# The last token tile of a trunk's last down projection: its tail products by halves of the columns, with the sum and the square of each half behind it

## The chip, the core and the metric

The kernel runs on one core of one Trainium2 chip, as one program. The metric is the device time of one execution in microseconds, the median of the timed runs. A profiled execution of the same program gives the trace; its span runs from the first instruction to the last. TensorE is called PE, its weight loads PEld, VectorE DVE, ScalarE ACT, GpSimd POOL and SyncE SP.

## The reference

A trunk of two layers over 512 tokens and 1024 channels, in float32. Each layer is a token mixer and a SwiGLU FFN, and each of these four ends in a gated RMSNorm that is added to the running `x`. Only the last step of the last FFN matters here:

```python
def rms_norm(x, g):
    xf = x.astype(jnp.float32)
    y = xf * lax.rsqrt(jnp.mean(xf * xf, axis=-1, keepdims=True) + EPS)
    return (y * g.astype(jnp.float32)).astype(x.dtype)

def swiglu(h, w_gate, w_up, w_down):
    return (jax.nn.silu(h @ w_gate) * (h @ w_up)) @ w_down
...
        y = swiglu(h, ffn_w_gate[i], ffn_w_up[i], ffn_w_down[i])
        x = x + gate * rms_norm(y, ffn_post_g[i])
    return x
```

`D_FF` is 2816, so the down projection has a contraction of 22 tiles of 128. The mean of the squares runs over all 1024 columns of a token: no column of the output can be scaled before the last square of its token is in.

## The kernel before

Matrices are multiplied in float32r, each operand split into a high and a low part; a product is three matmuls (`mm3`: high by high, high by low, low by high). The last FFN is `Ffn.last` (line 1255). Its down projection works on pairs of contraction tiles (11 pairs) and on the columns in two passes: pass `q = 0`, then `q = 1`, 512 columns each. The 512 columns of a pass are two groups of 256 (`h`), since the columns are laid out as `(h q c)`: half `h`, pass `q`, 256 columns.

In each pass eight PSUM banks are open, `Z`, `W`, `X` and `Y` for two token groups `s` (256 tokens each). Six of the eleven pairs in pass 1 go through a seven-product scheme of Winograd's kind (`seven`), the others through plain products (`eight`). The sums `Z` and `W`, which several outputs share, go to the tile `u` in `common` (line 1326). The last three pairs of pass 1 (`NLAST = 3`) are plain, and are kept back as `tail`: they are multiplied token tile by token tile, after everything else. There are four token tiles of 128 tokens (`tt`): tile `tt` has the bank `X` (even) or `Y` (odd) of the group `s = tt // 2`. For one token tile the tail is 3 pairs × 2 contraction tiles × 3 matmuls = 18 matmuls of 128x512 into one bank.

Behind the tail of each tile in pass 1 comes its finish, in this order in the code: `whole` adds bank and `u` into `y` on DVE and squares `y` on ACT with a running sum (`sq`; the squared values go to `junk` and are not used); `rms` (line 467) makes the sum of pass 0, scaled, the bias of a square root (`ss`, a DVE operation on 128x1) and takes that root on ACT (`sd`); `weigh` multiplies the kept half of pass 0 and then the new half by the weights `G` (`z`); a reciprocal on DVE gives `r`; two DVE operations add `r` times each half to `x`; each is followed by a DMA of its half of `x` to the output on SP's queue.

What sets the order: in this part no order is written out by hand. Each engine runs its own instructions one after the other as they stand in the built program. Between engines the framework places semaphore waits from the regions of tiles that instructions read and write. The listings below show, in square brackets, on which engine's semaphore a row waits.

Of the kernel before, what the change touches and what calls it, by code (L numbers as in the profile page):

```python
# [8 lines left out]
F32 = mybir.dt.float32  # L9
# [4 lines left out]
P = 128  # L14
T = 512
NT = T // P
# [17 lines left out]
def trunk(ctx: ExitStack, tc: tile.TileContext, A: dict, out: bass.AP):  # L34
# [17 lines left out]
    def nm(s):  # L52
        uid[0] += 1
        return f"{s}_{uid[0]}"
# [65 lines left out]
    def mm3(o, lh, ll, rh, rl, start, stop):  # L120
        mm(o, lh, rh, start, False)
        mm(o, lh, rl, False, False)
        mm(o, ll, rh, False, stop)

    def load(dst, src):
        nc.sync.dma_start(out=dst, in_=src)
# [1015 lines left out]
    class Ffn:  # L1142
# [112 lines left out]
        def last(self, bg0):  # L1255

            self.units(bg0)
            G = ada["G", 3].rearrange("p (h q c) -> p h q c", h=2, q=2)
            kept = {}

            def operands(q, p):

                a = self.act[p]
                t = slot(F32R, "ah"), slot(F32R, "al")
                split(t[0][:], t[1][:], a[:])  # L1270

                def A(e, c):
                    return lambda s: [
                        u[:, c, s * 256 + e * P : s * 256 + e * P + P] for u in t
                    ]

                ops = {f"A{e + 1}{c + 1}": A(e, c) for e in range(2) for c in range(2)}
                if p not in SEVEN[q]:
                    return ops
                if p not in kept:  # L1280
                    f = slot(F32, "S", 4, 256)
                    kept[p] = f
                    v = a[:].rearrange("p c (s e t) -> p c s e t", s=2, e=2)
                    S1, S2, S3, S4 = [
                        f[:, i, :].rearrange("p (s t) -> p s t", s=2) for i in range(4)
                    ]
                    dve.tensor_tensor(S1, v[:, 0, :, 1, :], v[:, 1, :, 1, :], ALU.add)
                    dve.tensor_tensor(S2, S1, v[:, 0, :, 0, :], ALU.subtract)
                    dve.tensor_tensor(S3, v[:, 0, :, 1, :], v[:, 0, :, 0, :], ALU.subtract)
                    dve.tensor_tensor(S4, v[:, 1, :, 0, :], S2, ALU.subtract)  # L1290
                f = kept[p]
                g = slot(F32R, "Sh", 4, 256), slot(F32R, "Sl", 4, 256)
                split(g[0][:], g[1][:], f[:])

                def S(i):
                    return lambda s: [u[:, i, s * P : (s + 1) * P] for u in g]

                ops.update({f"S{i + 1}": S(i) for i in range(4)})
                return ops

            def eight(p, O, W, banks, s, es, start):

                w = [[t[:, 2 * c : 2 * c + 2, :] for t in W] for c in range(2)]
                for e in es:
                    for c in range(2):
                        h, l = O[f"A{e + 1}{c + 1}"](s)
                        o = banks["XY"[e], s][:].rearrange("p (h c) -> p h c", h=2)
                        mm3(o, h, l, w[c][0], w[c][1], start and c == 0, False)

            SUMS = (  # L1310
                ("Z", 0, "A11", "B11"), ("W", 0, "S1", "T1"), ("Z", 1, "S2", "T2"),
                ("W", 1, "S3", "T3"), ("X", 0, "A12", "B21"), ("X", 1, "S4", "B22"),
                ("Y", 0, "A22", "T4"),
            )

            def seven(O, W, banks, fresh):
                for n, i, a, b in SUMS:
                    for s in range(2):
                        h, l = O[a](s)
                        mm3(  # L1320
                            banks[n, s][:, i * 256 : (i + 1) * 256], h, l, *W[b],
                            (n, s) in fresh, False,
                        )
                        fresh.discard((n, s))

            def common(banks):

                us = []
                for s in range(2):
                    u = fpool.tile([P, 4, 256], F32, tag="f13", name=nm("u"))  # L1330
                    z = [banks["Z", s][:, i * 256 : (i + 1) * 256] for i in range(2)]
                    w = [banks["W", s][:, i * 256 : (i + 1) * 256] for i in range(2)]
                    act.activation(u[:, 0, :], z[0], AF.Copy)
                    dve.tensor_tensor(u[:, 3, :], z[1], u[:, 0, :], ALU.add)
                    dve.tensor_tensor(u[:, 1, :], w[0], u[:, 3, :], ALU.add)
                    dve.tensor_tensor(u[:, 2, :], w[1], u[:, 3, :], ALU.add)
                    dve.tensor_tensor(u[:, 3, :], w[0], u[:, 2, :], ALU.add)
                    us.append(u)
                return us

            def whole(us, banks, tt, q):

                s, e = tt // 2, tt % 2
                y = ys[q, s][:, e, :]
                u = us[s][:, 2 * e : 2 * e + 2, :].rearrange("p a c -> p (a c)")
                dve.tensor_tensor(y, banks["XY"[e], s][:], u, ALU.add)
                sq = small.tile([P, 1], F32, tag=f"sq{q}{tt}", bufs=1, name=nm("sq"))
                act.activation(junk[:, q * 512 : (q + 1) * 512], y, AF.Square, accum_out=sq[:])
                yv = y.rearrange("p (h c) -> p h c", h=2)
                return sq, yv  # L1350

            def weigh(yv, q, out=None):
                dve.tensor_tensor(yv if out is None else out, yv, G[:, :, q, :], ALU.mult)

            ys = {}
            half = {}
            xs = []
            O = operands(0, PAIRS[0][0])
            for q in range(2):
                banks = {(n, s): bank(n, "p" if n == "W" else "b") for n in "ZWXY" for s in range(2)}  # L1360
                fresh = set(banks)
                tail = []
                us = None
                for n, p in enumerate(PAIRS[q]):
                    W = wget(("wdn", q, p), 2)
                    now = O
                    if n + 1 < NF or q == 0:
                        O = operands(*((q, PAIRS[q][n + 1]) if n + 1 < NF else (1, PAIRS[1][0])))
                    if p in SEVEN[q]:
                        seven(now, W, banks, fresh)  # L1370
                        if p == [i for i in PAIRS[q] if i in SEVEN[q]][-1]:
                            us = common(banks)
                    elif q == 1 and n >= NF - NLAST:
                        tail.append((p, now, W))
                    else:
                        for s in range(2):
                            eight(p, now, W, banks, s, (0, 1), ("X", s) in fresh)
                            fresh -= {("X", s), ("Y", s)}
                    if q == 1 and 0 <= n - 3 < NT:
                        xs.append(x_load(n - 3))  # L1380
                    if q == 1 and n == NF - NLAST - 2:
                        sqrt_table()
                for s in range(2):
                    ys[q, s] = slot(F32, "y")
                for tt in range(NT):
                    for t in tail:
                        eight(*t, banks, tt // 2, (tt % 2,), False)
                    if q == 0:
                        half[tt] = whole(us, banks, tt, 0)
                        continue  # L1390
                    sq, yv = whole(us, banks, tt, 1)
                    sd, r = rms(sq[:], half[tt][0][:])
                    weigh(half[tt][1], 0)
                    z = fpool.tile([P, 768], F32, tag="e", name=nm("z"))[:, :512]
                    z = z.rearrange("p (h c) -> p h c", h=2)
                    weigh(yv, 1, z)
                    dve.reciprocal(r[:], sd[:])
                    x = xs[tt].rearrange("p (h q c) -> p h q c", h=2, q=2)
                    o = out[tt * P : (tt + 1) * P, :].rearrange("p (h q c) -> p h q c", h=2, q=2)
                    for i, t in enumerate((half[tt][1], z)):  # L1400
                        dve.scalar_tensor_tensor(
                            x[:, :, i, :], t, r[:, 0:1], x[:, :, i, :], ALU.mult, ALU.add
                        )
                        load(o[:, :, i, :], x[:, :, i, :])


    u4 = []
# [269 lines left out]
```

## Time and profile before

| | us |
|---|---|
| timed runs | 1106.73, 1106.87, 1106.84; median 1106.84 |
| the profiled execution, span | 1104.6 |
| median of the runs less that span | 2.2 |
| PE busy in the span | 1085.9 (98%) |
| DVE busy | 945.9 (86%) |
| ACT busy | 594.2 (54%) |
| mean granted PE clock (share of full speed) | 0.998 |

The profile lists no time for the profiled execution outside its span; a timed run is 2.2 us longer than the span, which is what lies around the first and the last instruction. PE is busy nearly always, so what counts at the end of the kernel is when PE ends, and what has still to run behind it. In the views a row of the timeline is start, duration, engine, line, operation, output and inputs. Nearly every operation goes through a helper, so line 109 is any matmul, line 71 any DVE operation and line 87 any ACT operation: the tile names tell them apart. A durations row by form reads shortest/median/longest in ns.

### The profile page before, as it was taken

To read this page: it belongs to the slowest core of one execution; us is meant where nothing else is said; L and a number is where in the kernel's file an instruction comes from. 1 tells how busy PE (TensorE), PEld (TensorE's weight loads), DVE (VectorE), ACT (ScalarE), POOL (GpSimd) and SP (SyncE) were. 2 spreads that over 40 slices of the span, in tenths; PEclk is the share of its full clock that TensorE was granted. 3 is DMA by queue.
4 is the path that set the end of the run, shared out by engine and by line. 5 is a ranking of instruction groups with operands and counts; after the bars stand their busy time and mean duration, and the time that the engine had idled before them with its cause. 6 is when DMAs were issued, how large, how long until landed. Compare 5 with 4: busy or idle time off the path is not lost.

```text
span 1104.6 us, 18512 instructions
## 1 busy us (share of the span) xinstructions
PE 1085.9 (98%) x7404; PEld 979.0 (89%) x7404; DVE 945.9 (86%) x1248; ACT 594.2 (54%) x982; POOL 29.5 (3%) x53
## 2 busy tenths in 40 slices
PE   6999999999999999999999999999999999999997
PEld 4787788788999999998888889988999999989996
DVE  4988999966989999989866967668979999899997
ACT  6554665665655555554243626426555555565662
POOL 0020100000000000000000000001000000000000
PEclk9999999999999999999999999999999999999999
DMA  8976434304433434359757465334334343333252
GB/s 302 370 226 217 142 116 133 125 11 152 157 112 131 162 119 146 132 197 351 272 191 256 144 205 196 96 116 155 128 117 155 128 159 102 110 115 96 77 187 81
DMA packets 51355, 176.38 MB, mean 160 GB/s; under 512 B 6074, under 2 KB 9146, under 8 KB 51268
## 3 DMA queue, kind: packets, MB, share of 16 engines
q1 hardware_dynamic: 48708, 166.81, 44.6%
q0 software_dynamic: 2560, 8.39, 2.1%
q8 instruction: 58, 0.95, 0.3%
q14 instruction: 29, 0.24, 0.1%
HBM read 164.69 MB, written 8.39 MB: 157 GB/s over the span
## 4 chain that ended last, share of the span: by engine, by line
PE 90%; DVE 4%; DMA 2%; ACT 2%; issue 1%; SPq 0%; DVEq 0%; ACTq 0%
PE r L109 32%; PE y L109 18%; PE pqk L109 7%; PE gu L109 6%; PE v L109 5%; PE X L109 4%; PE u L109 4%; PE Y L109 3%; PE av L109 2%; PE z L109 2%; PE tw L117 1%; PE tp L117 1%; PE Z L109 1%; PE W L109 1%; PE ab L109 1%
## 5 line engine op out<-in xcount | busy, mean ns | idle before, releaser
L87 ACT ACTIVATE wh<-raw 128x1024 fp32r<-128x1024 f32 (+1 forms) x112 | 115.7, 1038 | 130.5 <-PE y L109 39.4
L109 PE MATMUL r<-Sh,wh 128*128 128x256 f32 x608 | 168.1, 276 | 0.5 <-ACT e L87 0.5
L109 PE MATMUL r<-Sh,wl 128*128 128x256 f32 x608 | 167.9, 276 | 0.0
L109 PE MATMUL r<-Sl,wh 128*128 128x256 f32 x608 | 167.9, 276 | 0.0
L109 PE MATMUL y<-wh,as 128*128 128x512 f32 x480 | 149.9, 390 | 0.0
L178 DVE TENSOR_TENSOR wl<-raw,wh 128x1024 fp32r<-128x1024 f32 x87 | 105.8, 1222 | 48.2 <-ACT wh L87 47.6
L109 PEld LDWEIGHTS r<-Sh,wh 128*128 128x128 f32 x608 | 114.1, 188 | 1.0 <-ACT e L87 0.9
L109 PEld LDWEIGHTS r<-Sl,wh 128*128 128x128 f32 x608 | 114.1, 188 | 0.1
L109 PEld LDWEIGHTS r<-Sh,wl 128*128 128x128 f32 x608 | 114.1, 188 | 0.0
L109 PEld LDWEIGHTS y<-wh,as 128*128 128x128 f32 x480 | 90.0, 188 | 18.6
L71 DVE TENSOR_TENSOR wl<-f,wh 128x1024 fp32r<-128x1024 f32 x87 | 103.2, 1220 | 0.0
L87 ACT ACTIVATE wh<-f 128x1024 fp32r<-128x1024 f32 x87 | 91.8, 1055 | 15.3 <-DVE f L71 11.6
L87 ACT ACTIVATE e<-r 128x256 f32<-128x256 f32 x114 | 43.7, 385 | 101.8 <-PE r L109 100.8
L109 PE MATMUL y<-wl,as 128*128 128x512 f32 x240 | 93.7, 391 | 0.0
L109 PE MATMUL r<-hTh,wh 128*128 128x256 f32 x304 | 84.2, 277 | 0.2 <-DVE gu L71 0.2
L109 PE MATMUL r<-hTl,wh 128*128 128x256 f32 x304 | 84.0, 276 | 0.0
L109 PE MATMUL r<-hTh,wl 128*128 128x256 f32 x304 | 84.0, 276 | 0.0
L109 PE MATMUL r<-hTh,b 128*128 128x256 f32 x304 | 57.9, 276 | 0.0
L109 PEld LDWEIGHTS r<-hTh,wh 128*128 128x128 f32 x304 | 57.1, 188 | 0.9 <-DVE gu L71 0.9
L109 PEld LDWEIGHTS r<-hTh,wl 128*128 128x128 f32 x304 | 57.1, 188 | 0.0
L109 PEld LDWEIGHTS r<-hTl,wh 128*128 128x128 f32 x304 | 57.1, 188 | 0.0
L87 ACT ACTIVATE wh<-rawx 128x1024 fp32r<-128x1024 f32 x38 | 40.4, 1063 | 29.8 <-PE r L109 29.0
(262 smaller groups left out, 2937.1 us busy)
## 6 DMA issues: line engine op xcount, KB each, us to landing
rawada<-in_ada SPq DMA_DIRECT2D x80, 512.0 KB, 5.7
rawy<-in_wy SPq DMA_DIRECT2D x38, 512.0 KB, 4.6
rawx<-in_wx SPq DMA_DIRECT2D x38, 512.0 KB, 3.7
raw<-in_wdown SPq DMA_DIRECT2D x22, 512.0 KB, 5.4
raw<-in_wdn SPq DMA_DIRECT2D x22, 512.0 KB, 3.6
raw<-in_wqk SPq DMA_DIRECT2D x16, 512.0 KB, 3.9
ada<-in_ada0p SPq DMA_DIRECT2D x12, 512.0 KB, 6.3
raw<-in_wgu SPq DMA_DIRECT2D x12, 512.0 KB, 3.5
```

What stands on the lines that cost most here:

```text
L71: b = getattr(nc.vector, op)(*args, **kw)
L87: b = nc.scalar.activation(*args, **kw)
L109: b = nc.tensor.matmul(o, l, r, start=start, stop=stop, skip_group_check=True)
L117: last_tp[0] = nc.tensor.transpose(o, i, ident)
L178: last_low[0] = nc.vector.tensor_tensor(l[:], raw[:], h[:].bitcast(F32), ALU.subtract)
```

## The change

For the last token tile of pass 1 alone (`tt = 3`) a function of its own, `last_tile`, takes the place of the common path. It runs the tail for the first 256 columns, then the sum and the square of these, then the tail for the other 256 columns, then their sum and square. `eight` gets a place `at` and a width `n` within the bank for that. The sum of the first half's squares is added to that of pass 0 (one more 128x1 operation on DVE), and `rms` takes this as its first part. The weighing is done by halves too. The last part (`finish`) is moved to a function and is the same.

```diff
-            def eight(p, O, W, banks, s, es, start):
+            def eight(p, O, W, banks, s, es, start, at=0, n=2):
 
-                w = [[t[:, 2 * c : 2 * c + 2, :] for t in W] for c in range(2)]
+                w = [[t[:, 2 * c + at : 2 * c + at + n, :] for t in W] for c in range(2)]
...
-                        mm3(o, h, l, w[c][0], w[c][1], start and c == 0, False)
+                        mm3(o[:, at : at + n], h, l, w[c][0], w[c][1], start and c == 0, False)
...
+            def last_tile(tail, us, banks, tt):
+                s, e = tt // 2, tt % 2
+                y = ys[1, s][:, e, :].rearrange("p (h c) -> p h c", h=2)
+                z = fpool.tile([P, 768], F32, tag="e", name=nm("z"))[:, :512]
+                z = z.rearrange("p (h c) -> p h c", h=2)
+                sq = [half[tt][0]]
+                weigh(half[tt][1], 0)
+                for h in range(2):
+                    for t in tail:
+                        eight(*t, banks, s, (e,), False, h, 1)
+                    dve.tensor_tensor(
+                        y[:, h, :], banks["XY"[e], s][:, h * 256 : (h + 1) * 256],
+                        us[s][:, 2 * e + h, :], ALU.add,
+                    )
+                    part = small.tile([P, 1], F32, tag="sq13" if h else "sq0", bufs=1 if h else None, name=nm("sq"))
+                    act.activation(
+                        junk[:, 512 + h * 256 : 768 + h * 256], y[:, h, :], AF.Square,
+                        accum_out=part[:],
+                    )
+                    if h == 0:
+                        dve.tensor_tensor(part[:], part[:], sq[0][:], ALU.add)
+                    sq.append(part)
+                    dve.tensor_tensor(z[:, h, :], y[:, h, :], G[:, h, 1, :], ALU.mult)
+                sd, r = rms(sq[2][:], sq[1][:])
+                dve.reciprocal(r[:], sd[:])
+                finish(tt, z, r)
...
                 for tt in range(NT):
+                    if q == 1 and tt == NT - 1:
+                        last_tile(tail, us, banks, tt)
+                        continue
```

On PE, at the end of the third tile's tail and the start of the fourth's (`X` is the third tile's bank, `Y` the fourth's, `wh`/`wl` and `ah`/`al` the high and low parts of weights and activations), there stood before:

```order
L109 MATMUL X_11315<-wl_11779,ah_11786 128x512
L109 MATMUL X_11315<-wh_11778,al_11787 128x512
L109 MATMUL Y_11317<-wh_11650,ah_11718 128x512
L109 MATMUL Y_11317<-wl_11651,ah_11718 128x512
L109 MATMUL Y_11317<-wh_11650,al_11719 128x512
```

and in the middle of the fourth tile's tail, where its first half ends and its second begins, there stand now:

```order
L109 MATMUL Y_11317<-wl_11779,ah_11786 128x256
L109 MATMUL Y_11317<-wh_11778,al_11787 128x256
L109 MATMUL Y_11317<-wh_11650,ah_11718 128x256 [waits DVE_49]
L109 MATMUL Y_11317<-wl_11651,ah_11718 128x256
L109 MATMUL Y_11317<-wh_11650,al_11719 128x256
```

The 18 matmuls of 128x512 have become 36 of 128x256, with the weights and activations of the first 18 used over again by the other 18. The nineteenth waits for DVE; no matmul of this tail waited for another engine before. In the built program the count on which it waits is the one that DVE's sum of the first half brings.

On DVE, the end of the program, from the third tile's last part on (`x_11646` belongs to the third tile, `x_11709` to the fourth, `y_11297` is the half of pass 0), before:

```order
L71 SCALAR_TENSOR_TENSOR x_11646<-z_11887,r_11885,x_11646 128x2x256
L71 TENSOR_TENSOR y_11791<-Y_11317,u_11770 128x512 [waits PE_49]
L71 TENSOR_TENSOR z_11921<-y_11791,G_8534 128x512 [waits DVE_49]
L71 RECIPROCAL r_11919<-sd_11917 128x1 [waits Activation_49]
L71 SCALAR_TENSOR_TENSOR x_11709<-y_11297,r_11919,x_11709 128x2x256 [waits DMAHW3_49,DVE_49]
L71 SCALAR_TENSOR_TENSOR x_11709<-z_11921,r_11919,x_11709 128x2x256
```

and now:

```order
L71 SCALAR_TENSOR_TENSOR x_11646<-z_11887,r_11885,x_11646 128x2x256
L71 TENSOR_TENSOR y_11791<-Y_11317,u_11770 128x256 [waits PE_49]
L71 TENSOR_TENSOR z_11894<-y_11791,G_8534 128x256 [waits DVE_49]
L71 TENSOR_TENSOR sq_11915<-sq_11915,sq_11308 128x1 [waits Activation_49]
L71 TENSOR_SCALAR ss_11941<-sq_11915 128x1 [waits DVE_49]
L71 TENSOR_TENSOR y_11791<-Y_11317,u_11770 128x256 [waits PE_49]
L71 TENSOR_TENSOR z_11894<-y_11791,G_8534 128x256 [waits DVE_49]
L71 RECIPROCAL r_11945<-sd_11943 128x1 [waits Activation_49]
L71 SCALAR_TENSOR_TENSOR x_11709<-y_11297,r_11945,x_11709 128x2x256 [waits DMAHW3_49,DVE_49]
L71 SCALAR_TENSOR_TENSOR x_11709<-z_11894,r_11945,x_11709 128x2x256
```

The sum and the weighing have become two each. The scaling `ss`, which stood ahead of all four tails, stands between the two sums now, with the new 128x1 sum before it, and both wait for ACT's first square. The first sum stands behind the third tile's two operations on `x`, as the whole sum did.

On ACT, the last squares and roots, before:

```order
L87 ACTIVATE sd_11849<-sq_11845,ss_11847 128x1 [waits Activation_49]
L87 ACTIVATE junk,sq_11879<-y_11791 128x512 [waits DVE_49]
L87 ACTIVATE sd_11883<-sq_11879,ss_11881 128x1 [waits Activation_49]
L87 ACTIVATE junk,sq_11913<-y_11791 128x512 [waits DVE_49]
L87 ACTIVATE sd_11917<-sq_11913,ss_11915 128x1 [waits Activation_49]
```

and now:

```order
L87 ACTIVATE junk,sq_11879<-y_11791 128x512 [waits DVE_49]
L87 ACTIVATE sd_11883<-sq_11879,ss_11881 128x1 [waits Activation_49]
L87 ACTIVATE junk,sq_11915<-y_11791 128x256 [waits DVE_49]
L87 ACTIVATE junk,sq_11938<-y_11791 128x256 [waits DVE_49]
L87 ACTIVATE sd_11943<-sq_11938,ss_11941 128x1 [waits Activation_49]
```

One square has become two of half the width. POOL's and SP's queues hold the same operations in the same order as before, the two DMAs of the last tile's output at the end among them.

More of the change, by code (lines that the diff above doesn't have):

```diff
@@ L1353, in weigh, with finish @@
                 dve.tensor_tensor(yv if out is None else out, yv, G[:, :, q, :], ALU.mult)
+            def finish(tt, z, r):
+                x = xs[tt].rearrange("p (h q c) -> p h q c", h=2, q=2)
+                o = out[tt * P : (tt + 1) * P, :].rearrange("p (h q c) -> p h q c", h=2, q=2)
+                for i, t in enumerate((half[tt][1], z)):
+                    dve.scalar_tensor_tensor(
+                        x[:, :, i, :], t, r[:, 0:1], x[:, :, i, :], ALU.mult, ALU.add
+                    )
+                    load(o[:, :, i, :], x[:, :, i, :])
+            def last_tile(tail, us, banks, tt):
[16 more added lines that the diff above has]
+                        accum_out=part[:],
+                    )
+                    if h == 0:
[5 more added lines that the diff above has]
+                finish(tt, z, r)
             ys = {}
@@ L1397, in last @@
                     dve.reciprocal(r[:], sd[:])
[L1398 to L1404, printed above, removed]
+                    finish(tt, z, r)
     u4 = []
```

## The prediction

> **What bounds the kernel now.** I read the page's busy shares first, then the chain of waits over the last 35 us, then the timelines of PE, DVE and ACT there. The share first:
>
> ```profile
> PE 1085.9 (98%) x7404; PEld 979.0 (89%) x7404; DVE 945.9 (86%) x1248; ACT 594.2 (54%) x982; POOL 29.5 (3%) x53
> ```
>
> PE has some 19 us without work in 1104.6, so a matmul more or a wait on PE is time, unless it falls where PE is idle. The chain that ended last (start, us, what) tells what stands behind PE:
>
> ```profile
> 1079.09 1.41 PE X L109 x12
> ...
> 1093.45 4.09 PE Y L109 x18
> 1097.54 0.02 issue
> 1097.57 0.70 DVE y L71
> 1098.27 0.02 issue
> 1098.29 0.73 ACT junk L87 x2
> 1099.03 0.02 issue
> 1099.05 0.30 ACT sd L87
> 1099.35 0.02 issue
> 1099.38 0.17 DVE r L71
> 1099.55 0.02 issue
> 1099.57 0.75 DVE x L71
> ```
>
> The fourth tile's 18 products are on the chain in one piece to 1097.54. Behind them stand the sum, the square, the root, the reciprocal and the two operations on `x`, each ended by the one ahead. What can be gained by halves is in two rows: the sum (0.70) and the square (0.73), since only the second half of each would stay behind PE. The rest, and the output's DMAs, wait for the root in either case.
>
> Now the DVE timeline around the fourth tile, from the third tile's sum on:
>
> ```profile
> 1093.49 0.69 DVE L71 TENSOR_TENSOR y<-X,u 128x512 f32<-128x512 f32 x1 [0.66 <-PE X L109]
> 1094.21 0.69 DVE L71 TENSOR_TENSOR z<-y,G 128x512 f32<-128x512 f32 x1
> 1095.30 0.17 DVE L71 RECIPROCAL r<-sd 128x1 f32<-128x1 f32 x1 [0.39 <-ACT sd L87]
> 1095.50 0.75 DVE L71 SCALAR_TENSOR_TENSOR x<-y,r,x 128x512 f32<-128x512 f32 x1
> 1096.16 0.74 DVE L71 SCALAR_TENSOR_TENSOR x<-z,r,x 128x512 f32<-128x512 f32 x1
> 1097.57 0.69 DVE L71 TENSOR_TENSOR y<-Y,u 128x512 f32<-128x512 f32 x1 [0.66 <-PE Y L109]
> ...
> 1100.24 0.75 DVE L71 SCALAR_TENSOR_TENSOR x<-z,r,x 128x512 f32<-128x512 f32 x1
> ```
>
> While PE multiplies the fourth tile, DVE finishes the third, and has only 0.66 us free between 1096.90 and 1097.57. With the whole tile in one piece this did not matter. It does once something on PE has to wait for DVE in the middle of the tail, as the changed program has it: the nineteenth matmul waits for DVE's sum of the first half.
>
> **The change part by part.** *Twice as many matmuls.* Two rows of the PE timeline, the first and the last of the fourth tile's 18:
>
> ```profile
> 1093.29 0.39 PE L109 MATMUL Y<-wh,ah 128*128 128x512 f32 x1
> ...
> 1097.14 0.39 PE L109 MATMUL Y<-wh,al 128*128 128x512 f32 x1
> ```
>
> They start (1097.14 − 1093.29) / 17 = 0.2265 us apart. Matmuls of 128x256 with a weight load each take 1.41 / 12 = 0.1175 (first row of the chain above), so two halves cost 0.235 in place of 0.2265: 18 × 0.0085 = +0.15 us on PE if nothing waits. The first half's 18 would start at 1093.29, since nothing ahead on PE changes, and the last of them at 1093.29 + 17 × 0.1175 = 1095.29. With 0.28 for it (row below) the first half is done at 1095.57.
>
> *The wait of the second half.* DVE can't take the first sum at 1095.57: it stands behind the third tile's two operations on `x`. These follow each other 0.66 apart (1095.50, 1096.16), so the sum starts some 0.66 after the second, at 1096.82; at the latest, with no overlap and a wake-up, at 1096.93. A sum of this width with an operand in PSUM is in the rows by form (shortest, median, longest in ns):
>
> ```profile
> L71 DVE TENSOR_TENSOR u<-W,u x12: 412/415/418, 1034.1 to 1083.7; 128x256 f32<-128x256 f32 x12
> ```
>
> and PE's restart behind a DVE read of the bank it writes next is at one place in the timeline, ahead of the down projection:
>
> ```profile
> 982.23 0.41 DVE L71 TENSOR_TENSOR gu<-e,r 128x256 f32<-128x256 f32 x1
> 982.70 0.19 PEld L109 LDWEIGHTS r<-hTh,wh 128*128 128x128 f32 x1 [0.64 <-DVE gu L71]
> 982.70 0.39 PE L109 MATMUL r<-hTh,wh 128*128 128x256 f32 x1 [0.21 <-DVE gu L71]
> 982.93 0.28 PE L109 MATMUL r<-hTl,wh 128*128 128x256 f32 x1
> 983.05 0.28 PE L109 MATMUL r<-hTh,wl 128*128 128x256 f32 x1
> ```
>
> The first sum takes 0.415 and ends at 1097.24. In the rows at 982 DVE's read ended at 982.64 and PE's weight load began at 982.70, 0.06 later; the load waited too, so PE can't get it out of the way. The first matmul after that cost 0.23 to the second's start, the others 0.12 as ever. So the second half's load starts at 1097.30, its second matmul at 1097.53, the eighteenth 16 × 0.1175 = 1.88 later at 1099.41, and it ends at 1099.69. Before, PE ended at 1097.14 + 0.39 = 1097.53. That is +2.16 us, and PE idles for 1.73 us from 1095.57 on. Nothing stands behind the waiting matmul on PE but the tail itself, and the first to wait for that is the second sum. The row at 982 only shows a wait for a read of the same columns that are written next.
>
> [...]
>
> *The sum, in two.* The second sum starts 0.04 behind PE, as before (1097.53, 1097.57). Its 0.415 for 0.69 takes 0.28 off the chain.
>
> *The square, in two.* No square of 256 columns is in the trace. ACT's groups by form (busy us, mean ns; the first from the last 24 us alone):
>
> ```profile
> L87 ACT ACTIVATE junk<-y 128x512 bf16<-128x512 f32 x4 | 2.5, 632 | 15.0 <-DVE y L71 15.0
> L87 ACT ACTIVATE gu<-gu 128x256 f32<-128x256 f32 x38 | 15.5, 407 | 2.2 <-DVE gu L71 2.2
> L87 ACT ACTIVATE as<-act 128x512 fp32r<-128x512 f32 x22 | 12.8, 620 | 0.0
> ```
>
> ACT's rows from SBUF to SBUF fall from 620 at 512 to 407 at 256, which is 0.21. The bounds are 0.32, half of the square's 632, and 0, if none of it scaled. I take 0.21, for the gap of those two rows is that of a like operation on the same engine. The read-out of the accumulator stays once behind the second square, and the root behind it.
>
> *Small ones.* A DVE operation on 128x1 is short, as the scaling of this tile was:
>
> ```profile
> 1084.08 0.14 DVE L71 TENSOR_SCALAR ss<-sq 128x1 f32<-128x1 f32 x1
> ```
>
> The new 128x1 sum waits for ACT's first square. That starts at 1097.27 and, with its accumulator's read-out, takes the 0.76 from square to root in the chain less 0.21, so 0.55, to 1097.82. With the scaling behind it DVE is through by 1098.1, while PE works to 1099.69: the second half's matmuls hide both, and the first weighing. If PE did not wait, the two would be late (second rival). The second weighing runs beside the second square and root, as the whole one did. The scaling taken from ahead of the tails frees DVE where it waits anyway. POOL and SP have the same queues, and the last tile's two output DMAs start later by whatever `x` does.
>
> *Sum:* +2.16 (PE) − 0.28 (sum) − 0.21 (square) = **+1.67 us**. The last operation on `x` moves from 1100.24 to 1101.91, and the span from 1104.6 to 1106.3. A run is 2.2 us longer than the span, so the median 1106.84 becomes 1108.51. Its own bounds: −0.11 (square halved), +0.21 (square not scaled), +0.11 (DVE starts late), some 0.1 either way for the restart, so 1108.2 to 1108.9.
>
> **The rivals.** *The clock falls in the wait.* PE idles for 1.73 us in the middle of its tail. The windows with the granted clock at the end of the trace, where PE stopped at 1097.53:
>
> ```profile
> 1100.50:1101.00 0.50, 0.00 (x0) 0.00 (x0) 0.49 (x1) 0.00 (x0) 0.00 (x0) 1.00 0.00 0
> 1101.00:1101.50 0.50, 0.00 (x0) 0.00 (x0) 0.00 (x0) 0.00 (x0) 0.00 (x0) 0.56 0.00 0
> 1101.50:1102.00 0.50, 0.00 (x0) 0.00 (x0) 0.00 (x0) 0.00 (x0) 0.00 (x0) 0.50 0.86 293
> ```
>
> The clock (the column after the five engines) stayed at 1.00 for some 3.5 us without matmuls, then fell to 0.50. An idle time of half that length speaks against a fall, but the trace has no idle of 1 to 3 us before more matmuls. If it did fall at once, 18 matmuls would take twice 0.1175: +2.1 us, 1110.6, slower by 0.34%. It decides once it costs over 0.54 us (1109.05 is 0.2% above the median), that is from 5 slow matmuls on. This rival ends on the other side of the forecast.
>
> [...]
>
> *The second half does not wait long*, because its matmuls run on while DVE is busy, or the wait is for something done. PE would end at 1093.29 + 35 × 0.1175 + 0.28 = 1097.68. But DVE runs in order: the first sum to 1097.24, then the 128x1 sum behind the square at 1097.82, then the scaling, so that the second sum starts at about 1098.1, 0.5 later than before, and 0.28 + 0.21 come off again: 1106.85, no change. Without even that it would be +0.15 − 0.49 = −0.34, 1106.5. The wait in the program and DVE's third tile speak against both.
>
> *Faster by over 0.2%* needs 2.2 us off, and the two rows that the change halves come to 1.43 in all.
>
> **How the numbers follow.** 0.2% is 2.2 us, about what a measurement of this kernel can tell from no change. The forecast, 1108.51 or +0.15%, lies within it: chance 0.86. Clock falls or a restart that costs at least 0.54 more: 0.08, near 1110. Little or no wait: 0.06, from 1106.5 to 1106.9. 0.03 of the forecast's 0.86 is for its upper end to lie above 1109.05, and 0.01 of the last case for a gain over 0.2%: faster 0.01, same 0.83 + 0.05 = 0.88, slower 0.08 + 0.03 = 0.11. The likeliest case has 1108.2 to 1108.9; with 0.2 us for the timed runs and for errors in what follows PE the range is 1107.9 to 1109.1, and it leaves both rivals' own times out.
>
> **What would show it.** In the profile after: 18 matmuls of 128x256 ending near 1095.6; the nineteenth's weight load with an idle time of about 1.7 put down to DVE `y`, at 1097.3; a first sum of 0.41 at 1096.8 right behind the third tile's second `x`; the second sum near 1099.7; a square of about 0.42 in place of 0.63; a clock of 1.00 over 1095 to 1100. I am wrong if PE runs through the tail with no gap, if the matmuls after the gap are more than 0.13 apart, or if the first sum starts before 1096.8.

## The result, and the profile after

| | before | after |
|---|---|---|
| median of 21 runs, us | 1106.34 (1104.07 to 1107.87) | 1107.97 (1105.70 to 1109.61) |
| ratio | | 1.0014, 95% interval 1.0009 to 1.0020 |
| the profiled execution: span, us | 1104.6 | 1105.1 |
| tail: first matmul of the fourth tile to the start of the last operation on `x` | 1093.29 to 1100.24: 6.95 us | 1092.09 to 1100.73: 8.64 us |

The changed kernel is slower by 0.14%, 1.6 us. Single executions of either kernel scatter by some 4 us, and the two profiled ones differ by 1.2 us before the fourth tile begins, over PE code that is the same. So the spans say little. The length of the tail is read from one trace of each kernel, and it is used below to compare kernels. Two timed executions of the experiments' kernels took far longer than all others, 1578 us (own bank) and 2203 us (a wait between); nothing here explains them, and the ratios below leave them out.

The chain of waits of the changed kernel, from the third tile's operations on `x`:

```profile
1094.30 1.41 DVE x L71 x2
1095.71 0.35 DVE y L71
1096.06 0.04 issue
1096.10 2.42 PE Y L109 x18
1098.52 0.02 issue
1098.54 0.44 DVE y L71
1098.98 0.02 issue
1099.00 0.52 ACT junk L87 x2
1099.52 0.02 issue
1099.54 0.30 ACT sd L87
...
1100.07 0.75 DVE x L71
```

Before, this chain ran over PE alone to 1097.54. Now it leaves PE for DVE in the middle of the tail: the third tile's `x`, the first half's sum, and only then the second half's 18 matmuls. The sum (0.44) and the square with its read-out (0.52) behind them are shorter than the 0.70 and 0.73 of before.

The timelines of PE and of its weight loads, the first half's first and last matmul and the second half's start:

```profile
1092.09 0.28 PE L109 MATMUL Y<-wh,ah 128*128 128x256 f32 x1
...
1094.12 0.28 PE L109 MATMUL Y<-wh,al 128*128 128x256 f32 x1
1096.10 0.38 PE L109 MATMUL Y<-wh,ah 128*128 128x256 f32 x1 [1.70 <-DVE y L71]
1096.32 0.28 PE L109 MATMUL Y<-wl,ah 128*128 128x256 f32 x1
...
1098.23 0.28 PE L109 MATMUL Y<-wh,al 128*128 128x256 f32 x1
```

```profile
1096.10 0.19 PEld L109 LDWEIGHTS Y<-wh,ah 128*128 128x128 f32 x1 [1.90 <-DVE y L71]
```

PE stands still for 1.70 us and the trace names DVE's `y`. The weight load waited too, and began with the matmul at 1096.10. On DVE:

```profile
1094.96 0.75 DVE L71 SCALAR_TENSOR_TENSOR x<-z,r,x 128x512 f32<-128x512 f32 x1
1095.63 0.42 DVE L71 TENSOR_TENSOR y<-Y,u 128x256 f32<-128x256 f32 x1
1096.08 0.42 DVE L71 TENSOR_TENSOR z<-y,G 128x256 f32<-128x256 f32 x1
...
1096.81 0.15 DVE L71 TENSOR_SCALAR ss<-sq 128x1 f32<-128x1 f32 x1
1098.54 0.42 DVE L71 TENSOR_TENSOR y<-Y,u 128x256 f32<-128x256 f32 x1 [1.58 <-PE Y L109]
```

The first half was there at 1094.40, DVE took it at 1095.63, right behind the third tile's second `x`. Then DVE itself waited 1.58 us for PE. On ACT the two squares took 0.42 each, where the whole one took 0.63:

```profile
1096.08 0.42 ACT L87 ACTIVATE junk<-y 128x256 bf16<-128x256 f32 x1 [2.01 <-DVE y L71]
1099.00 0.42 ACT L87 ACTIVATE junk<-y 128x256 bf16<-128x256 f32 x1 [2.41 <-DVE y L71]
```

The clock, in windows over the first half, the gap and the second half (a row has the window, its length, the busy time of PE, PEld, DVE, ACT and POOL, then the granted clock, the DMA share and GB/s):

```profile
1092.09:1094.40 2.31, 2.31 (x19) 2.10 (x17) 1.65 (x4) 1.02 (x3) 0.00 (x0) 1.00 0.66 227
1094.40:1096.10 1.70, 0.00 (x1) 0.00 (x1) 1.67 (x4) 0.02 (x1) 0.00 (x0) 1.00 0.00 0
1096.10:1098.52 2.42, 2.40 (x18) 2.20 (x18) 0.72 (x3) 0.49 (x2) 0.00 (x0) 1.00 0.63 217
```

It stayed at 1.00 in this execution. All 21 runs have a mean clock of 0.998 or 0.999, as those of the kernel before have beside the experiments. A fall of 3.4 us at 0.50, as the kernel with a wait between has it below (1098.10 to 1101.50), would take 0.0015 off (an estimate: half of 3.4 in 1108), so by that the 15 runs at 0.999 had no such fall; the six at 0.998 don't rule it out, but they are not the longer ones (1107.6 on average, against 1108.1).

### The profile page after: what moved, and what is told of

Same layout as the page of the kernel before. It is cut to its first block, busy times and chain, and to the rows that moved or that the text cites. A ratio compares the mean times of both kernels' runs of the same rounds, so it can differ in the third digit from the quotient of the medians.

```text
span 1105.1 us, 18553 instructions
## 1 busy us (share of the span) xinstructions
PE 1085.1 (98%) x7422; PEld 979.5 (89%) x7422; DVE 946.1 (86%) x1251; ACT 595.1 (54%) x984; POOL 29.5 (3%) x53
## 4 chain that ended last, share of the span: by engine, by line
PE 89%; DVE 5%; DMA 2%; ACT 2%; issue 1%; SPq 0%; DVEq 0%; ACTq 0%
PE r L109 31%; PE y L109 18%; PE pqk L109 7%; PE gu L109 6%; PE v L109 5%; PE X L109 4%; PE u L109 4%; PE Y L109 3%; PE av L109 2%; PE z L109 2%; PE tw L117 1%; PE tp L117 1%; PE Z L109 1%; PE W L109 1%; PE ab L109 1%
```

## The experiments

In this section the tail is what the table above defines: 6.95 us before, 8.64 after. Ratios are to the kernel before, run beside on the same chip.

**A bank of its own for the second half.** The bank `Y` already holds the second half's sum of the earlier pairs; this is added to `u` ahead of the four tails, and the second half's tail starts afresh in `Z`, whose content is used up by then.

```diff
-                    for t in tail:
-                        eight(*t, banks, s, (e,), False, h, 1)
+                    to = {("Y", 1): banks["Z" if h else "Y", 1]}
+                    for i, t in enumerate(tail):
+                        eight(*t, to, s, (e,), h == 1 and i == 0, h, 1)
...
-                        y[:, h, :], banks["XY"[e], s][:, h * 256 : (h + 1) * 256],
+                        y[:, h, :], to["Y", 1][:, h * 256 : (h + 1) * 256],
...
+                if q == 1:
+                    u1 = us[1][:, 3, :]
+                    dve.tensor_tensor(u1, banks["Y", 1][:, 256:512], u1, ALU.add)
```

> The changed kernel, but the second half's 18 products go to a bank of their own (Z of the same token group, free by then), and what the bank Y holds of the second half is added to u ahead of the four tails. Measure: the tail, from the first matmul of the fourth tile to the start of the last operation on x, 6.95 us before (1093.29 to 1100.24) and 8.64 after (1092.09 to 1100.73). Theory (PE waits because DVE's first sum reads the bank it writes next, and DVE is late by the third tile): no gap on PE; 36 matmuls 0.12 apart end 4.45 after the first, the second sum starts at about 4.7, since the 128x1 sum ahead of it on DVE waits for ACT's first square, and the tail is 6.85 to 6.95; 1.7 less than after, time as before within 0.1%. Rival (the split itself costs, by twice the matmuls and operations): the tail stays above 8, time 0.1 to 0.2% above before. Rival (the time went ahead of the tail): the tail is as the theory says but the time stays 1.5 us above before.

Measured: ratio 0.9998 (0.9988 to 1.0008). The tail is 6.80 (1094.20 to 1101.00), 0.05 below the range named. PE's timeline has no gap at the seam:

```profile
1096.23 0.28 PE L109 MATMUL Y<-wh,al 128*128 128x256 f32 x1
1096.35 0.28 PE L109 MATMUL Z<-wh,ah 128*128 128x256 f32 x1
...
1098.39 0.28 PE L109 MATMUL Z<-wh,al 128*128 128x256 f32 x1
```

and DVE's queue holds the second sum instead, for a short while:

```profile
1097.74 0.42 DVE L71 TENSOR_TENSOR y<-Y,u 128x256 f32<-128x256 f32 x1
1098.19 0.42 DVE L71 TENSOR_TENSOR z<-y,G 128x256 f32<-128x256 f32 x1
1098.73 0.16 DVE L71 TENSOR_TENSOR sq<-sq,sq 128x1 f32<-128x1 f32 x1
1098.81 0.42 DVE L71 TENSOR_TENSOR y<-Z,u 128x256 f32<-128x256 f32 x1
```

PE was done at 1098.67; the second sum came 0.14 later, behind the 128x1 sum. The matmuls are the same 36, there is one sum more ahead of the tails, and the tail is 1.84 us shorter than the changed kernel's: the split itself doesn't cost it, and the time did not go ahead of the tail. But for that sum, what the two kernels differ in is the bank.

**The same, with the 128x1 sum behind the second sum.**

```diff
-                    if h == 0:
-                        dve.tensor_tensor(part[:], part[:], sq[0][:], ALU.add)
+                    if h == 1:
+                        both = dve.tensor_tensor(sq[1][:], sq[1][:], sq[0][:], ALU.add)
+                        order(both, add)
```

(`add` is the second half's sum.)

> As the kernel with the bank of its own, and the 128x1 sum of the squares placed behind the second sum on DVE. Theory (what is left is DVE's queue): the second sum starts 4.49 after the first matmul, 0.04 behind PE, and the tail is 6.7, 0.25 below before; in time that is 0.02%, not to be told from before. Rival (the split itself costs): a tail above 8, time 0.1 to 0.2% above before.

Measured: ratio 0.9994 (0.9985 to 1.0004), tail 6.74 (1093.20 to 1099.94). The second sum starts 4.51 after the first matmul, 0.04 behind PE's last one. It is the shortest tail of all, 0.2 below before; as a time it can't be told from before, though its median, 1105.95, is the lowest.

**The products alone by halves.** The tail of the fourth tile runs as two times 18 matmuls of 128x256 into one bank; the sum and all else as before.

```diff
+                    for h in range(2 if q == 1 and tt == NT - 1 else 0):
+                        for t in tail:
+                            eight(*t, banks, tt // 2, (tt % 2,), False, h, 1)
+                    for t in tail if q == 0 or tt < NT - 1 else ():
                         eight(*t, banks, tt // 2, (tt % 2,), False)
```

> The kernel before with the fourth tile's products alone by halves: 36 matmuls of 128x256 into one bank, no sum between, and then the whole sum and square as before. Theory (the wait costs, not the matmuls): no gap on PE, 36 matmuls end 4.45 after the first in place of 4.24, and the tail is 7.16, 0.2 above before; time within 0.1% of before. Rival (twice the matmuls cost the time): PE's end at 6 or more and a tail of 8.4 or more, time 0.1 to 0.2% above before.

Measured: ratio 1.0007 (0.9998 to 1.0016), tail 7.19 (1094.81 to 1102.00). The chain:

```profile
1094.97 4.32 PE Y L109 x36
1099.30 0.02 issue
1099.32 0.70 DVE y L71
```

36 matmuls in one piece, 4.32 where 18 wide ones took 4.09. Twice the matmuls cost 0.24 of the tail.

**The first sum ahead of the third tile's `x`.** The bank is the same; `finish` of the third tile is called behind the first half's sum, and its two operations on `x` are ordered behind that (`add`).

```diff
+                    if h == 0:
+                        finish(*before, add)
```

> The changed kernel, same bank, but on DVE the first half's sum stands ahead of the third tile's two operations on x. Theory (the length of the wait is set by DVE's queue, its being there by the bank): the gap on PE stays, but falls from 1.70 to about 0.5 us (the sum's 0.42, and 0.1 of wake-ups); the second half ends 5.25 after the first matmul and the tail is 7.4 to 7.5: 0.5 above before, 1.2 below after. Rival (a restart of PE costs a fixed time): the gap stays near 1.7 and the tail near 8.6. Rival (the sum does not hold PE): no gap, tail 6.9.

Measured: ratio 1.0005 (0.9996 to 1.0015), tail 7.48 (1093.77 to 1101.25). The chain, and the second half's first matmul:

```profile
1093.93 2.16 PE Y L109 x18
1096.09 0.02 issue
1096.12 0.43 DVE y L71
1096.55 0.04 issue
1096.59 2.43 PE Y L109 x18
```

```profile
1096.59 0.39 PE L109 MATMUL Y<-wh,ah 128*128 128x256 f32 x1 [0.52 <-DVE y L71]
```

The gap is there still, 0.52 us, about as long as the sum with the two short delays (0.02 and 0.04) around it. With the first sum reading the bank that PE writes next there is a gap, 1.70 and here 0.52, and with two banks there was none. So the shared bank brings the wait, and DVE's queue makes its length: 1.2 of the changed kernel's 1.70 us were the third tile.

**The sum and the square alone by halves.** The products are whole.

```diff
+                for t in tail:
+                    eight(*t, banks, s, (e,), False)
                 for h in range(2):
-                    for t in tail:
-                        eight(*t, banks, s, (e,), False, h, 1)
```

> The fourth tile's products whole, 18 of 128x512 as before, and only what stands behind them by halves: two sums, two squares, two weighings. Theory (halves pay only where the first half's sum and square run beside PE): the first square starts 0.3 earlier than before, but the second has to wait for the first one's read-out, and the root starts 0.05 to 0.15 later than before; the tail is 7.0 to 7.1 against 6.95, time as before. Rival (sum and square overlap and that is the gain of the change): a tail of 6.7 or less.

Measured: ratio 0.9998 (0.9989 to 1.0007), tail 7.13 (1093.94 to 1101.07), 0.03 above the range named. The root:

```profile
1099.88 0.29 ACT L87 ACTIVATE sd<-sq,ss 128x1 f32<-128x1 f32 x1 [0.29 <-DVE ss L71]
```

In this order the halves gain nothing behind PE, but not for the reason expected: the root waited for the scaling (`ss`), which stands last on DVE, and not for ACT's read-outs, which were done at 1099.59. Without that wait of 0.29 the tail would be about 6.85, 0.1 below before (an estimate from these rows, not tried). So this run doesn't show what halves behind PE could gain with `ss` out of the way.

**A longer wait.** One DVE operation of 128x1024 that nobody needs stands ahead of the first sum, ordered behind the third tile's last `x`:

```diff
+                    for i in range(1 if h == 0 else 0):
+                        f = fpool.tile([P, 4, 256], F32, tag="f24", bufs=1, name=nm("idle"))
+                        g = ada["G", 3].rearrange("p (a b) -> p a b", a=4)
+                        b = dve.tensor_tensor(f[:], g, g, ALU.mult)
+                        order(b, prev)
+                        prev = b
...
+                    if h == 0:
+                        order(add, prev)
```

> The changed kernel with one more DVE operation of 128x1024, whose result nobody reads, between the third tile's last operation on x and the first half's sum. Theory (PE waits for that sum, one for one): the gap on PE grows from 1.70 by 1.15 to about 2.85, the tail from 8.64 to 9.8; the granted clock stays at 1.00 and the second half's matmuls 0.12 apart. Rival (the wait is for something else than DVE's queue): gap and tail as in the changed kernel. Rival (the clock falls in such a wait): matmuls 0.2 apart or more behind the gap and a tail of 11 or more.

Measured in one execution: the gap was 2.83 as the theory has it, but the tail 11.10 (1092.33 to 1103.43), as the clock's rival has it. The windows of the gap, the matmuls at once behind it, and the rest:

```profile
1094.65:1097.48 2.83, 0.00 (x0) 0.00 (x1) 2.80 (x5) 0.02 (x1) 0.00 (x0) 1.00 0.34 115
1097.48:1098.10 0.62, 0.62 (x5) 0.62 (x6) 0.50 (x2) 0.49 (x2) 0.00 (x0) 1.00 0.93 319
1098.10:1101.20 3.10, 3.10 (x16) 2.81 (x14) 0.21 (x2) 0.00 (x0) 0.00 (x0) 0.50 0.00 1
```

The clock fell 0.6 us after PE had gone on (1097.48, 1098.10), and the matmuls went from 0.12 to 0.21 apart. So I was wrong to expect 1.00 behind a gap of 2.8 us because the kernel before had kept it for some 3.5 us at its end.

**A long wait.** The same with five such operations.

> As the kernel with the longer wait, with five such operations. Theory (one for one): the gap is 7.5 to 8 us and the tail at least 14.6. That is over twice the 3.5 us after which the granted clock fell at the end of the kernel before, so the clock should fall to 0.50 inside the gap, and the second half's 18 matmuls should take 4.3 in place of 2.4: tail 16.5 to 17. Rival (the clock does not fall in a wait ahead of more matmuls): 0.12 apart, tail 14.7.

Measured in one execution: the gap was 7.87, the clock 0.50 from 1096.54 on, inside the gap (0.77 is the mean over the first row below), and the 18 matmuls took 4.23. The tail is 16.63 (1091.17 to 1107.80), as expected.

```profile
1096.00:1097.00 1.00, 0.00 (x0) 0.00 (x0) 1.00 (x1) 0.00 (x0) 0.00 (x0) 0.77 0.86 309
1101.30:1105.60 4.30, 4.21 (x18) 3.92 (x18) 0.74 (x3) 0.51 (x2) 0.00 (x0) 0.50 0.00 0
```

**A wait between.** The same with one operation of 128x512.

> The changed kernel with one more DVE operation of 128x512, whose result nobody reads, ahead of the first half's sum: a gap on PE of about 2.3 us, between the changed kernel's 1.70 and the 2.83 at which the granted clock fell to 0.50 for 3.4 us after PE had gone on. [...]

The gap was 2.30, and the clock fell here too, to 0.50 from 1098.10, 0.26 us after PE had gone on: ratio 1.0028 (1.0017 to 1.0039), tail 10.76 (1093.22 to 1103.98). 5 of 6 runs have a mean clock of 0.997. The fall itself is seen in the profiled one alone; one run of the kernel with its own bank, which has no gap, has 0.997 too, so a mean is a sign and no proof.

```profile
1095.54:1097.84 2.30, 0.00 (x1) 0.01 (x1) 2.27 (x5) 0.02 (x1) 0.00 (x0) 1.00 0.18 62
1097.84:1098.10 0.26, 0.26 (x2) 0.26 (x3) 0.26 (x1) 0.26 (x1) 0.00 (x0) 1.00 1.03 347
1098.10:1101.50 3.40, 3.40 (x18) 3.40 (x17) 0.45 (x3) 0.23 (x2) 0.00 (x0) 0.50 0.25 86
1101.50:1104.90 3.40, 0.25 (x2) 0.05 (x1) 2.43 (x5) 0.81 (x3) 0.00 (x0) 1.00 0.00 0
```

**The longer wait again, many times.**

> The kernel with the gap of 2.83 us once more, many times. [...] Rival (the fall comes each time): all runs at 0.997, time 0.35% above before.

Ratio 1.0032 (1.0023 to 1.0041). In 3 of 11 runs the mean clock is 0.998, in 8 it is 0.995 to 0.997. The profiled execution was one where it held; same kernel, same gap:

```profile
1094.52:1097.35 2.83, 0.00 (x1) 0.00 (x0) 2.80 (x5) 0.02 (x1) 0.00 (x0) 1.00 0.34 114
1097.35:1099.80 2.45, 2.41 (x18) 2.20 (x18) 0.72 (x4) 0.49 (x2) 0.00 (x0) 1.00 0.22 82
```

Its tail is 9.78 (1092.21 to 1101.99), the 9.8 that the wait alone makes. So the fall came in one profiled execution and not in the other, with the same kernel and the same gap of 2.83. The times don't part into two groups, as the scatter of the executions (some 4 us) is wider than the step between the two tails (1.32); sorted by the mean clock, the 3 runs at 0.998 take 1108.3 on average and the 8 others 1110.2. Two of these have 0.995, at least 10 us at half clock (an estimate: 0.0045 of 1108 us, twice), against 6.3 in the profile of the longer wait, its end included. No profile shows such an execution, so where the rest lies stays open.

## Why the prediction was right or wrong

*The sum was right, term by term.* PE's gap was to be 1.73 and was 1.70. The first sum was to start 3.53 after the fourth tile's first matmul and started 3.54 after it. From there: second half's end 6.42 after the first matmul (6.40 foretold), second sum 0.42 (0.415), square to root 0.54 (0.55). The tail grew by 1.69 us, against +1.67.

*The likeliest case was the one that came; the absolute time was too high.* The three runs shown before the change lay at 1106.84, the 21 have 1106.34. So 1108.51 was foretold and 1107.97 measured; the difference of the medians is 1.63. The measured time lies below the likeliest 1108.2 to 1108.9, and only just above 1107.9. That is in part luck: the bounds named come to 1108.3 (1108.51 − 0.11 − 0.1), and with 0.2 off to 1108.1, while the three runs alone were off by 0.5. The 2.2 us between a run and its span, which compared two different executions, are 1.72 to 1.85 in every run listed with its own span; the forecast's difference doesn't hang on it.

*The step that failed is the one that took 0.2% for about what a measurement can tell from no change.* It put a forecast of +0.15% down as "same", with 0.88. No row of the prediction stood behind that. Single executions scatter by some 4 us, but the medians of 21 runs each give a ratio to about ±0.055%, 0.6 us. The interval, 1.0009 to 1.0020, leaves 1 out: this is a slower kernel, by 1.6 us, about what the sum had said. The mechanism was sized and then called nothing, where "slower by 1.67 us, which twenty runs of each can show" was the forecast that the working bore.

*The rival of the clock* did not come at 1.70 us in the trace, and the mean clocks show no sign of it. But the reason given, that an idle time of half of 3.5 us speaks against a fall, was weak. At 2.30 us, 0.6 more, the profiled execution has it and 5 of 6 runs have a mean clock of 0.997. There the tail was about 1.5 us longer than the wait alone makes it (10.76 against 8.64 + 0.60, an estimate). The price had been put too high: at a clock of 0.50 the matmuls of the long wait lie 0.21 apart and not 0.235, and the 18 of them took 4.23 in place of 2.42, so 1.8 and not 2.1.

*The rival without a wait* did not come, since the wait is in the program. With a bank of its own it gave a tail 0.15 to 0.21 below before, between the two values worked out for it (no change, and 0.34 below). What is shown is that the wait (1.70 us in one bank) goes when the second half goes to another bank (no gap at the seam, 1096.23 to 1096.35). It stood although the columns that DVE reads and those that PE writes next are not the same, so what the program guards is wider than the columns. Whether the chip could read and write other columns of one bank at once was not tried. Nor does a run here show what would happen in one bank without the wait.

*Where the expected gain went:* the halves take 0.49 off behind PE, and 0.24 goes to PE for twice the matmuls. That leaves 0.25 at best, and 0.2 is what the best version got. The wait then costs 1.70, and 0.24 more goes to PE's running empty and its restart (6.42 to the second half's end, against 4.48 in one piece). Together that is 1.69, what the tail grew by.

## What to carry to other kernels

In this program, splitting a product by columns let the vector work overlap only when the halves lay in different banks (no gap on PE). In one bank, PE waited until the reader was done, and the price was that reader's place in its queue, not its own duration (1.70 against 0.5 us). In a kernel of your own, look for such a wait in the built program. Before a wait is put into PE's stream, look up what stands ahead of the awaited instruction on its engine. And work out the best case first: here the sum and square that could be hidden came to 0.49 us, of which half went to the narrower matmuls.

## What the runs showed of the chip that I had not expected

The granted clock fell after PE had gone on working. In the kernel with the 2.30 us gap PE went on at 1097.84; the clock was 1.00 to 1098.10, 0.50 from there to 1101.50, and 1.00 from 1101.50 to 1104.90, although PE was busy for only 0.25 us of that last stretch. In the kernel with the longer gap PE went on at 1097.48, and the clock was 1.00 to 1098.10 and 0.50 over 1098.10 to 1101.20, behind a gap of 2.83 us. In the repeat a gap of 2.83 us was followed by 1.00 all through the second half (1097.35 to 1099.80).

From PE's stop to the fall the traces show different times: 2.56 us in the wait between (1095.54 to 1098.10), 3.45 in the longer wait (1094.65 to 1098.10) and about 3.1 in the long one (1093.48 to 1096.54). At the end of the trace, where no matmul follows, it was about 2.7 in the repeat (PE to 1099.78; 1.00 to 1102.50, 0.51 over 1102.50 to 1106.40), 3.5 in the kernel before (1097.54 to 1101.06) and 4.9 in the changed kernel (1098.52 to 1103.45). These times don't agree on one length of idle time. What the clock goes by was not shown, and so neither was how far the changed kernel's 1.70 us lay from a fall.
